# The second block of the input projection joins at step 5 in place of step 9, and its norm is put to the products

## The chip, the cores and the metric

The kernel runs on one core of a Trainium2 chip. The metric is the device time of one launch in microseconds (us). Before the change it is 2964.63 us, the median of three runs from 2958.12 to 2965.66. All traces here are of one profiled execution each.

## The reference, cut to what matters

One layer of a streaming encoder runs over 2128 tokens: 64 sample frames of a running stream, 16 meta tokens and 2048 prompt frames. What the change touches is the head of the layer:

```
h = x * rsqrt(mean(x*x) + EPS) * norm_mix_g        # one norm per token, one gain per feature
p = h @ W_in                                       # 1024 -> 2832 columns
q, k, v (attention) | lx, lg (RG-LRU) | gq, gk, gv, glr, gog (GLA) = split(p)
```

Then differential attention, the RG-LRU recurrence and the GLA recurrence work on their columns, `W_out` joins them, and a gated feed-forward network (FFN, 2816 wide, with a causal convolution) follows. A norm is one number per token, so it can be put either to `h` before the product or to the columns (or rows) of the product behind it.

## The kernel before, in words

Every matmul is done in three parts: each operand is split into a rounded high half and the rest (`hh`, `hl` for h; `whi`, `wlo` for a weight), and hh·whi, hl·whi and hh·wlo are added up in PSUM. A block of h has eight pieces of 128 features, so a unit (128 columns of `W_in` by one block) is 24 matmuls.

**W_in.** The 17 tiles of tokens (80 and 16 times 128) form six blocks, `WBLOCKS`, of 336, four times 384, and 256 tokens. The columns of `W_in` form 19 units, `UNITS` (line 87): eight `f` units for the recurrences' columns (stored to LGT), one `g` unit (three weight parts, GVR, tokens as rows), four `f` units of K, four of Q, and two `t` units of V (two weight parts, tokens as rows). `win` (from line 602) goes through steps; step s works on unit s mod 19. `WSTART` (line 94) says at which step a block joins, and a block stays for 19 steps. Blocks 0, 2, 4 use one pair of h tiles and join at steps 0, 22, 44; blocks 1, 3, 5 use the other and join at 9, 31, 53. A step with two live blocks puts one weight part to both. There are 72 steps.

**Weights.** Each step's part is loaded from HBM into one of two `raw` tiles (`w_load`), then split (`w_split`, lines 244 to 270): ScalarE writes `whi` (line 154), VectorE (line 160) or GpSimd (line 260, two of three) writes `wlo`. There are three slots of whi and wlo (`NW = 3`), so the `g` unit holds all three while it runs. All loads and stores are issued by SyncE (lines 148 and 151).

**Norms.** Block 0 uses `first_rows`: hh is x times the gain (line 496), hl the rest (497), squares are made on ScalarE (381) and added on VectorE (383), and the norm is put to the products later: `row_scale` for `g` and `t` units, `col_scale` for `f` units, so that block 0's `f` products leave PSUM by a VectorE multiply (`columns`, line 518), and the other blocks' by a ScalarE copy (520). All other blocks use `norm_in`: squares, adds on GpSimd, `rsqrt_rows` (lines 396 to 406), and then `normed` (438 to 445), which writes the scaled y and splits it into hh and hl. The raw x of a block lies in a single buffer (tile `x` of pool `xp`), so the next block's x is loaded (`load_x`) when the one before has been read for the last time. The norm of block i is begun by `win` three steps ahead or more: for i of 2 and above at the step after block i-2 has left, and for block 1 at step 1.

**Order.** Three streams (dense work, attention, recurrences) are written out by `Flow.run`, and the tile scheduler places their instructions on the engines by priority: attention and recurrences stand ahead of dense work by 30000 and 16000, `boost` puts a norm's instructions ahead by 50000, and block 0's by `FIRST`, 100000. Each engine then runs its own list strictly in that order. The recurrences' first chunk needs block 0's units 0 to 8, the attention its K, Q and V.

**After W_in.** W_out and the FFN of two groups of 512 tokens run beside the rest of the attention and the recurrences, and a last group of 1104 tokens runs alone.

Of the kernel before, what the change touches and what calls it, by code (L numbers as in the profile page):

```python
# [16 lines left out]
ALU = mybir.AluOpType  # L17
# [26 lines left out]
TILES = [(0, XW)] + [(XW + P * i, P) for i in range(SEQ // P)]  # L44
# [20 lines left out]
WBLOCKS = [[0, 1, 2], [3, 4, 5], [6, 7, 8], [9, 10, 11], [12, 13, 14], [15, 16]]  # L65
# [16 lines left out]
for _name, _w in (("gm", 8), ("gf", 8), ("gl", 8), ("lcw", 8), ("lcb", 2), ("lab", 2), ("lxb", 2), ("ll", 2), ("lsc", 6), ("lsh", 2),  # L82
# [6 lines left out]
UNITS = [("f", 1536), ("f", 1664), ("f", 1792), ("f", 1920), ("f", 2048), ("f", 2176), ("f", 2576), ("f", 2704),  # L89
         ("g", 2304)] + [("f", 512 + P * i) for i in range(4)] + [("f", P * i) for i in range(4)] + [("t", 1024), ("t", 1280)]  # L90
GVK = ((0, 3), (3, 6), (6, 8))


WSTART = [9 * (i % 2) + i // 2 * (len(UNITS) + 3) for i in range(len(WBLOCKS))]
WSTEPS = max(WSTART) + len(UNITS)


# [41 lines left out]
def tile_hymba_step(ctx, tc, xT, xkT, cache_v, wi, wo, wu, wg, wd, par, sgla, c_msk, yT_p, yT_s, nkT_p, nv_p, lh_p, lc_p, gs_p, fc_p,  # L139
                    nkT_s, nv_s, lh_s, lc_s, gs_s, fc_s):  # L140
    nc = tc.nc
# [5 lines left out]
    def ld(out, in_):  # L147
        nc.sync.dma_start(out=raw32(out), in_=raw32(in_))
# [138 lines left out]
    FIRST = 100000  # L287
# [70 lines left out]
    def boost(gen, off):  # L358

        on = off  # L360
        while True:
            tc.cur_priority -= on
            c = next(gen, "end")
            tc.cur_priority += on
            if c == "end":
                return
            on = off
            if isinstance(c, tuple):
                c, on = c[0], off * (off == FIRST)
            yield c  # L370
# [89 lines left out]
    x_ahead = {}  # L460

    def load_x(i, first=lambda: None):
        if i < len(WBLOCKS) and i not in x_ahead:
            n, tok0 = width(WBLOCKS[i]), TILES[WBLOCKS[i][0]][0]
            x_ahead[i] = xp.tile([P, KT, n], F32, tag="x", name="xt")
            step = 4 if i else 2
            for k in range(0, KT, step):
                ld(out=x_ahead[i][:, k:k + step], in_=xT[k:k + step, :, tok0:tok0 + n].rearrange("k p c -> p k c"))
                if k == 0:
                    first()  # L470

    def norm_in(i, H):
        load_x(i)
        n = width(WBLOCKS[i])
        x = x_ahead[i]
        acc = ev.tile([P, WMAX], F32, tag="acc", name="acc", bufs=1)
        for k in range(KT):
            add_square(acc, k, x[:, k], ev, True)
            if k % 2:
                yield 1000  # L480
        rb = []
        yield from rsqrt_rows(acc, n, ev, rb)
        yield from normed(rb, "gm", lambda k: x[:, k], ev, H)
        load_x(i + 1)

    row_scale, col_scale = {}, []

    def first_rows(H):

        x = x_ahead[0]  # L490
        blk = WBLOCKS[0]
        n = width(blk)
        acc = ev.tile([P, WMAX], F32, tag="acc", name="acc", bufs=1)
        for k in range(KT):
            hk, lk = H[0][:, k], H[1][:, k]
            nc.scalar.activation(out=hk, in_=x[:, k], func=AF.Copy, scale=pr("gm", k))
            nc.vector.scalar_tensor_tensor(out=lk, in0=x[:, k], scalar=pr("gm", k), in1=f(hk), op0=ALU.mult,
                                           op1=ALU.subtract)
            add_square(acc, k, x[:, k], ev)
        cuts = [(TILES[t][0], TILES[t][1]) for t in blk]  # L500
        ps = ps_t.tile([P, 4], F32, tag="t", name="ps_sq")
        for j, (o, w) in enumerate(cuts):
            nc.tensor.matmul(ps[:w, j:j + 1], lhsT=acc[:, o:o + w], rhs=ones[:, 0:1], start=True, stop=True)
        r = ev.tile([P, 4], F32, tag="r", name="r", bufs=2)
        row_norms(r, ps, cuts)
        for j, (t, (o, w)) in enumerate(zip(blk, cuts)):
            row_scale[t] = r[:w, j:j + 1]
        dg = ev.tile([P, WMAX], F32, tag="sq", name="dg", bufs=NSQ)
        pb = yield from spread(r, dg, cuts, ps_t, "t")
        rb = mp.tile([P, NMAX], F32, tag="pc", name="rb", bufs=2 * NPC)  # L510
        nc.vector.tensor_copy(rb[:, :n], pb[:, :n])
        col_scale.append(rb[:, :n])
        load_x(1)

    def columns(out, blk, ps):

        if blk[0] == 0:
            nc.vector.tensor_tensor(out, ps, col_scale[0], ALU.mult)
        else:
            nc.scalar.activation(out=out, in_=ps, func=AF.Copy)  # L520

# [19 lines left out]
    def put_q(h):  # L541
        def put(blk, tok0, n, ps):
            e = ev.tile([P, 2, WMAX], F32R, tag="e2", name="e_q", bufs=2)
            if blk[0] == 0:
                e1 = ev.tile([P, WMAX], F32, tag="ef", name="e_q1", bufs=3)
                columns(e1[:, :n], blk, ps[:, :n])
                ps = e1
            rounded(e[:, 0, :n], ps[:, :n], scale=-0.125)
            nc.vector.scalar_tensor_tensor(out=e[:, 1, :n], in0=ps[:, :n], scalar=-0.125, in1=f(e[:, 0, :n]),
                                           op0=ALU.mult, op1=ALU.subtract)  # L550
            st(QHL[h, :, :, :, tok0:tok0 + n].rearrange("l m d c -> (m d) l c"), e[:, :, :n])
        return put
# [55 lines left out]
    def win():  # L608
        H, norms = {}, {}
        for s_ in range(WSTEPS):  # L610
            u = s_ % len(UNITS)
            kind = UNITS[u][0]
            for i, blk in enumerate(WBLOCKS):

                if s_ == max(0, WSTART[i - 2] + len(UNITS)) if i >= 2 else s_ == i:
                    (H[i],) = h_tiles([width(blk)], hp, (f"hh{i % 2}_", f"hl{i % 2}_"))
                    norms[i] = boost(norm_in(i, H[i]), 50000) if i else boost(first_rows(H[i]), FIRST)
                if s_ == WSTART[i]:
                    yield from norms.pop(i)
            live = [i for i in range(len(WBLOCKS)) if WSTART[i] <= s_ < WSTART[i] + len(UNITS)]  # L620
            ranges = unit_parts(kind)
            wt = w_take(("in", s_), len(ranges))
            wd_ = unit_width(kind)

            def wview(k, l):
                for (a, b), pair in zip(ranges, wt):
                    if a <= k < b:
                        return pair[l][:, (k - a) * wd_:(k - a + 1) * wd_]
            for i in live:
                blk = WBLOCKS[i]  # L630
                b0 = TILES[blk[0]][0]
                for t in [None] if kind == "f" else blk:
                    if t is None:
                        c0, n = 0, width(blk)
                    else:
                        c0, n = TILES[t][0] - b0, TILES[t][1]
                    ps = ps_w.tile([P, NMAX], F32, tag="w", name="ps_w")
                    for k in range(KT):
                        for i3, (pa, pb) in enumerate(((0, 0), (0, 1), (1, 0))):
                            hx = H[i][pb][:, k, c0:c0 + n]  # L640
                            wx = wview(k, pa)
                            st_, sp_ = (k == 0 and i3 == 0), (k == KT - 1 and i3 == 2)
                            if t is None:
                                nc.tensor.matmul(ps[:, :n], lhsT=wx, rhs=hx, start=st_, stop=sp_)  # L644
                            else:
                                nc.tensor.matmul(ps[:n, :wd_], lhsT=hx, rhs=wx, start=st_, stop=sp_)  # L646
                        if k % 2 == 1:
                            w_pump()
                            if k == KT - 1:
                                if t is None:  # L650
                                    puts[u](blk, b0, n, ps)
                                else:
                                    puts[u](t, ps)
                            yield 6 * (n if t is None else wd_) * 0.425
                            yield from beside(norms)
                lg_done[i] = lg_done[i] or {(WSTART[i] + x) % len(UNITS) for x in range(s_ - WSTART[i] + 1)} >= set(range(9))
                win_done[i] = s_ == WSTART[i] + len(UNITS) - 1
            w_used(len(ranges))
            if s_ == 1:
                setup2()  # L660
            if s_ == 3:
                cached_keys()
                sample_masks()
# [315 lines left out]
    class Unit:  # L979
# [16 lines left out]
        def width(self, ti, ci):  # L996
            k0, kn = self.chunks[ci]
            return min(kn, self.n0 - k0) if not self.X and ti == 0 else kn
# [639 lines left out]
```

## Time and profile before

| | |
|---|---|
| median of three runs | 2964.63 us |
| profiled execution: time, span | 2966.77 us, 2965.0 us |
| mean granted TensorE clock | 0.979 |
| last matmul of W_in starts | 800.9 us |

In a row of instructions the columns are: start in us from the span's start, duration in us, engine, line, operation, out<-in, shapes, how many instructions the row merges, and in brackets the idle time of the engine before it with what ended it. PE is the matmul engine (TensorE), DVE is VectorE, ACT ScalarE, POOL GpSimd, SPq SyncE's queue. In a row of stretches: its length, the busy time of each engine with the number of instructions, the granted clock of TensorE (1.00 is 2.4 GHz, 0.5 would be 1.2 GHz throughout), the share of DMA and GB/s. In a row of groups: mean ns of one after the bar and the comma, then idle time before the group by releaser.

### The profile page before, as it was taken

The page shows a single profiled execution, that of the slowest core. Times are in us where ns is not written, and L with a number is a line of the kernel's source. Part 1 is how long each engine was busy: PE and PEld are TensorE (multiplying, and loading weights), DVE is VectorE, ACT ScalarE, POOL GpSimd, SP SyncE. Part 2 cuts the span into 40 slices and gives each one's busy share as a digit, 9 for nine tenths or more (in the row PEclk, how much of TensorE's full clock was granted, in tenths as well). Part 3 has the DMA queues.
Part 4 walks back from the last instruction along what each step waited for, and adds up shares of the span by engine and source line. Part 5 has one row for each costly group of instructions (what it writes and reads, how often), then busy time and mean ns, then how long its engine had stood idle before and what let it go on. Part 6 is the DMA issues. An engine that isn't in the chain of part 4 may idle for free.

```text
span 2965.0 us, 44672 instructions
## 1 busy us (share of the span) xinstructions
PE 2846.8 (96%) x16031; PEld 2508.9 (85%) x16031; DVE 1942.6 (66%) x3779; ACT 1140.1 (38%) x2589; POOL 864.2 (29%) x1212
## 2 busy tenths in 40 slices
PE   7999999999899999999999999999999999999998
PEld 7988899989877787787787888888989998999997
DVE  7677685788879989979979766444454333333335
ACT  5454554555555455455444433111222121212122
POOL 4435534444435445444424221100110000000001
PEclk9999999999998999999998999999999999999998
DMA  7775574655796787787775565675222222222222
GB/s 233 208 210 148 175 225 139 196 181 188 237 336 216 250 261 246 230 261 266 262 265 171 188 204 193 243 287 197 73 86 86 86 86 86 86 86 86 86 86 105
DMA packets 277931, 537.44 MB, mean 181 GB/s; under 512 B 31014, under 2 KB 170030, under 8 KB 277710
## 3 DMA queue, kind: packets, MB, share of 16 engines
q1 hardware_dynamic: 277566, 534.58, 54.7%
q8 instruction: 127, 2.08, 0.3%
q14 instruction: 94, 0.77, 0.1%
q10 hardware_dynamic: 144, 0.01, 0.0%
HBM read 382.74 MB, written 151.76 MB: 180 GB/s over the span
## 4 chain that ended last, share of the span: by engine, by line
PE 72%; DVE 15%; DMA 5%; issue 3%; ACT 3%; POOL 2%; SPq 1%; POOLq 0%; ACTq 0%; DVEq 0%
PE pu L1302 15%; PE pd L1369 15%; PE pg L1302 14%; PE pd L1437 6%; PE ps_w L644 5%; PE ps_w L646 4%; PE ps_o L1169 3%; DVE pc L1103 3%; PE ps_sc L1062 2%; PE ps_sc L1055 2%; PE ps_pt L1154 2%; DVE NB L1064 1%; PE ps_r L894 1%; DMA raw<-in_wi 1%; DVE cc L1326 1%
## 5 line engine op out<-in xcount | busy, mean ns | idle before, releaser
L260 POOL TENSOR_TENSOR wlo<-raw,whi 128x1024 fp32r<-128x1024 f32 (+1 forms) x104 | 248.1, 2387 | 315.8 <-ACT whi L154 263.9
L1326 DVE SCALAR_TENSOR_TENSOR cc<-uh,prm,cc 128x512 f32<-128x512 f32 (+4 forms) x264 | 168.3, 645 | 256.4 <-ACT cc L1324 253.4
L1065 ACT ACTIVATE pc<-ps_sc,NB 128x512 f32<-128x512 f32 (+6 forms) x400 | 224.8, 563 | 285.7 <-DVE NB L1064 244.6
L1369 PE MATMUL pd<-gh,whi 128*128 128x512 f32 (+2 forms) x880 | 317.7, 363 | 12.3 <-DVE x L1375 10.6
L1375 DVE TENSOR_TENSOR x<-x,pd 128x512 f32<-128x512 f32 (+2 forms) x320 | 195.8, 617 | 200.3 <-PE pd L1369 199.0
L1302 PE MATMUL pu<-h2h,whi 128*128 128x512 f32 (+2 forms) x880 | 319.9, 364 | 7.1 <-ACT h2h L154 2.6
L1302 PE MATMUL pu<-h2l,whi 128*128 128x512 f32 (+2 forms) x880 | 318.0, 362 | 3.6 <-POOL h2l L443 2.7
L1302 PE MATMUL pu<-h2h,wlo 128*128 128x512 f32 (+2 forms) x880 | 317.4, 361 | 0.0
L1302 PE MATMUL pg<-h2h,whi 128*128 128x512 f32 (+2 forms) x880 | 315.4, 358 | 1.7 <-DMA whi<-WS 1.7
L1302 PE MATMUL pg<-h2h,wlo 128*128 128x512 f32 (+2 forms) x880 | 315.7, 359 | 0.0
L1302 PE MATMUL pg<-h2l,whi 128*128 128x512 f32 (+2 forms) x880 | 315.2, 358 | 0.0
L1369 PE MATMUL pd<-gl,whi 128*128 128x512 f32 (+2 forms) x880 | 314.0, 358 | 0.0
L1369 PE MATMUL pd<-gh,wlo 128*128 128x512 f32 (+2 forms) x880 | 313.9, 357 | 0.0
L1319 ACT ACTIVATE uh<-pu 128x336 f32<-128x336 f32 (+3 forms) x132 | 59.3, 465 | 556.9 <-PE pu L1302 556.3
L644 PE MATMUL ps_w<-hh,whi 128*128 128x384 f32 (+2 forms) x768 | 257.7, 338 | 16.1 <-ACT whi L154 10.9
L1064 DVE TENSOR_REDUCE NB<-ps_sc 128x1 f32<-128x512 f32 (+6 forms) x400 | 209.0, 529 | 79.8 <-PE ps_sc L1062 78.8
L644 PE MATMUL ps_w<-hl,whi 128*128 128x384 f32 (+2 forms) x768 | 258.2, 337 | 0.5 <-DVE hl L160 0.5
L644 PE MATMUL ps_w<-hh,wlo 128*128 128x384 f32 (+2 forms) x768 | 254.8, 334 | 0.3 <-DVE wlo L160 0.3
L157 POOL TENSOR_SCALAR gh<-cc 128x336 fp32r<-128x336 f32 (+3 forms) x132 | 68.4, 520 | 468.8 <-DVE cc L1339 376.2
L154 ACT ACTIVATE whi<-raw 128x1024 fp32r<-128x1024 f32 (+2 forms) x160 | 165.9, 1037 | 101.6 <-DMA raw<-in_wi 31.3
L1369 PEld LDWEIGHTS pd<-gh,whi 128*128 128x128 f32 x880 | 166.3, 189 | 36.9 <-DVE x L1375 13.1
L1302 PEld LDWEIGHTS pu<-h2h,whi 128*128 128x128 f32 x880 | 168.6, 192 | 30.0 <-issue 3.0
(330 smaller groups left out, 7126.4 us busy)
## 6 DMA issues: line engine op xcount, KB each, us to landing
wlo<-WS SPq DMA_DIRECT2D x148, 512.0 KB, 4.3
whi<-WS SPq DMA_DIRECT2D x148, 512.0 KB, 4.5
raw<-in_wi SPq DMA_DIRECT2D x74, 512.0 KB, 4.5
WS<-whi SPq DMA_DIRECT2D x74, 512.0 KB, 5.1
WS<-wlo SPq DMA_DIRECT2D x74, 512.0 KB, 6.3
Kc<-KHL SPq DMA_DIRECT2D x48, 512.0 KB, 5.3
V<-VHL SPq DMA_DIRECT2D x48, 512.0 KB, 5.2
Q<-QHL SPq DMA_DIRECT2D x64, 256.0 KB, 4.3
```

Source lines behind the costliest of these rows:

```text
L154: nc.scalar.activation(out=out, in_=in_, func=AF.Copy, scale=scale)
L260: nc.gpsimd.tensor_tensor(out=lo[:, :n], in0=t[:, :n], in1=f(hi[:, :n]), op=ALU.subtract)
L644: nc.tensor.matmul(ps[:, :n], lhsT=wx, rhs=hx, start=st_, stop=sp_)
L646: nc.tensor.matmul(ps[:n, :wd_], lhsT=hx, rhs=wx, start=st_, stop=sp_)
L1064: nc.vector.tensor_reduce(NB[:qw, ti, m, ci:ci + 1], ps[:qw, :kt_], AX.X, ALU.min)
L1065: nc.scalar.activation(out=pv_[m][:qw, :kt_], in_=ps[:qw, :kt_], func=AF.Exp, scale=-1.0, bias=NB[:qw, ti, m, ci:ci + 1], accum_out=SS[:qw ...
L1103: nc.vector.scalar_tensor_tensor(out=p0, in0=p0, scalar=u.R[:qw, ti, 0, ci:ci + 1], in1=p1, op0=ALU.mult, op1=ALU.add)
L1302: nc.tensor.matmul(ps[:, :n], lhsT=w_[wi_][:, k * P:(k + 1) * P], rhs=hx, start=(k == 0 and i3 == 0), stop=(k == KT - 1 and i3 == 2))
L1326: nc.vector.scalar_tensor_tensor(out=cc[:, :m], in0=uh[:, w:w + m], scalar=cw[w], in1=cc[:, :m], op0=ALU.mult, op1=ALU.add)
L1369: nc.tensor.matmul(ps[:, :n], lhsT=w_, rhs=g_[:, o:o + n], start=(j == 0 and i3 == 0), stop=(j == len(gts) - 1 and i3 == 2))
L1375: nc.vector.tensor_tensor(x2[b, ct], x2[b, ct], ps[:, :n], ALU.add)
L1437: nc.tensor.matmul(ps[:, :n], lhsT=w_, rhs=g_, start=(k == 0 and i3 == 0), stop=(k == KT - 1 and i3 == 2))
```

## The change

`WSTART` puts blocks 1, 3 and 5 at steps 5, 27 and 49 in place of 9, 31 and 53; with that there are 68 steps. Block 1 gets `first_rows` too: its hh and hl are made from x and the gain alone, its adds of squares run on VectorE, its `f` products leave PSUM by `columns`' VectorE multiply, and its norms of rows and columns (`r`, `rb`) are kept until its last unit. The boost of block 1 stays at 50000. `load_x(2)` is called at the end of `first_rows` of block 1.

```
-WSTART = [9 * (i % 2) + i // 2 * (len(UNITS) + 3) for i in range(len(WBLOCKS))]
+WSTART = [5 * (i % 2) + i // 2 * (len(UNITS) + 3) for i in range(len(WBLOCKS))]
...
-    row_scale, col_scale = {}, []
-
-    def first_rows(H):
-
-        x = x_ahead[0]
-        blk = WBLOCKS[0]
+    row_scale, col_scale = {}, {}
+
+    def first_rows(i, H):
+
+        x = x_ahead[i]
+        blk = WBLOCKS[i]
...
-        cuts = [(TILES[t][0], TILES[t][1]) for t in blk]
+        cuts = [(TILES[t][0] - TILES[blk[0]][0], TILES[t][1]) for t in blk]
...
-        col_scale.append(rb[:, :n])
-        load_x(1)
+        col_scale[blk[0]] = rb[:, :n]
+        load_x(i + 1)
...
-        if blk[0] == 0:
-            nc.vector.tensor_tensor(out, ps, col_scale[0], ALU.mult)
+        if blk[0] in col_scale:
+            nc.vector.tensor_tensor(out, ps, col_scale[blk[0]], ALU.mult)
...
-            if blk[0] == 0:
+            if blk[0] in col_scale:
                 e1 = ev.tile([P, WMAX], F32, tag="ef", name="e_q1", bufs=3)
...
-                    norms[i] = boost(norm_in(i, H[i]), 50000) if i else boost(first_rows(H[i]), FIRST)
+                    norms[i] = boost(norm_in(i, H[i]), 50000) if i > 1 else boost(first_rows(i, H[i]), 50000 if i else FIRST)
```

## Rows read from the trace of the kernel before

**Rows 1.** The page, busy time of each engine over the span
```profile
PE 2846.8 (96%) x16031; PEld 2508.9 (85%) x16031; DVE 1942.6 (66%) x3779; ACT 1140.1 (38%) x2589; POOL 864.2 (29%) x1212
```

**Rows 2.** The table of stretches, by stage
```profile
800.00:1620.00 820.00, 773.24 (x3772) 629.71 (x3772) 720.39 (x1390) 420.64 (x973) 345.86 (x438) 0.96 0.76 253
1620.00:2965.00 1345.00, 1324.39 (x7396) 1171.43 (x7395) 624.64 (x1130) 310.52 (x614) 165.09 (x378) 0.99 0.37 131
```

**Rows 3.** The table of stretches, four tens of microseconds near the start
```profile
20.00:30.00 10.00, 8.79 (x56) 8.28 (x55) 9.68 (x20) 5.94 (x13) 8.93 (x10) 1.00 0.68 222
40.00:50.00 10.00, 10.00 (x59) 9.73 (x58) 2.91 (x8) 3.75 (x7) 4.73 (x3) 0.83 0.82 241
60.00:70.00 10.00, 4.05 (x16) 3.74 (x17) 8.69 (x15) 6.56 (x13) 6.30 (x5) 0.74 0.48 139
70.00:80.00 10.00, 10.00 (x57) 9.63 (x56) 7.05 (x18) 6.68 (x16) 5.96 (x8) 0.92 0.97 334
```

**Rows 4.** The timeline of PE, its idle times from 22 to 76 us
```profile
24.15 0.38 PE L318 MATMUL ps_lam<-lam_p,ones 64*128 64x2 f32 x2 [0.70 <-DVE rb L511]
...
39.47 0.45 PE L725 MATMUL ps_r<-xc,prm 128*128 128x83 f32 x2 [1.08 <-DVE xc L713]
...
53.36 0.35 PE L646 MATMUL ps_w<-whi,hh 128*80 128x272 f32 x1 [1.12 <-ACT whi L154]
...
63.96 0.42 PE L644 MATMUL ps_w<-hh,whi 128*128 128x336 f32 x1 [4.10 <-ACT whi L154]
...
66.86 0.38 PE L808 MATMUL ps_r<-ident,gvr 128*16 128x128 f32 x1 [1.99 <-DMA gvr<-GVR]
```

**Rows 5.** The timeline of PE, first matmuls of two units that follow each other
```profile
80.69 0.33 PE L644 MATMUL ps_w<-hh,whi 128*128 128x384 f32 x1
...
84.88 0.31 PE L644 MATMUL ps_w<-hh,whi 128*128 128x336 f32 x1
```

**Rows 6.** Groups of instructions, shapes apart, from 0 to 310 us
```profile
L260 POOL TENSOR_TENSOR wlo<-raw,whi 128x1024 fp32r<-128x1024 f32 x17 | 41.1, 2416 | 31.0 <-ACT whi L154 31.0
L154 ACT ACTIVATE whi<-raw 128x1024 fp32r<-128x1024 f32 x28 | 29.4, 1050 | 13.1 <-DMA raw<-in_wi 6.9 <-PE ps_w L644 5.2 <-PE ps_w L646 0.9
...
L381 ACT ACTIVATE sq<-xt 128x384 f32<-128x384 f32 x21 | 10.2, 512 | 0.8 <-POOL acc L383 0.8
...
L497 DVE SCALAR_TENSOR_TENSOR hl<-xt,prm,hh 128x336 fp32r<-128x336 f32 x8 | 4.4, 563 | 3.7 <-ACT hh L496 3.7
L496 ACT ACTIVATE hh<-xt,prm 128x336 fp32r<-128x336 f32 x8 | 4.2, 562 | 0.6 <-DMA xt<-in_xT 0.6
L518 DVE TENSOR_TENSOR e_lgt<-ps_w,rb 128x336 f32<-128x336 f32 x8 | 3.8, 500 | 0.0
...
L383 DVE TENSOR_TENSOR acc<-acc,sq 128x336 f32<-128x336 f32 x7 | 3.5, 500 | 0.1
```

**Rows 7.** The timeline of ACT, when block 1's x is there
```profile
18.87 0.52 ACT L381 ACTIVATE acc<-xt 128x384 f32<-128x384 f32 x1 [3.48 <-PE ps_sq L503]
21.36 1.06 ACT L154 ACTIVATE whi<-raw 128x1024 fp32r<-128x1024 f32 x1 [1.14 <-DMA raw<-in_wi]
```

**Rows 8.** The timeline of DVE from 20 to 62 us
```profile
24.13 1.34 DVE L518 TENSOR_TENSOR e_lgt<-ps_w,rb 128x336 f32<-128x336 f32 x3
...
53.45 2.77 DVE L438 SCALAR_TENSOR_TENSOR y<-xt,prm,acc 128x384 f32<-128x384 f32 x3
...
58.29 0.60 DVE L438 SCALAR_TENSOR_TENSOR y<-xt,prm,acc 128x384 f32<-128x384 f32 x1
```

**Rows 9.** Timelines of SPq, POOL, PE and ACT: block 3's load, squares and norm
```profile
245.72 0.92 SPq L148 DMA_DIRECT2D xt<-in_xT  x2
...
266.83 1.06 POOL L383 TENSOR_TENSOR acc<-acc,sq 128x384 f32<-128x384 f32 x1
...
321.38 0.72 PE L396 MATMUL ps_sq<-ones,acc 128*128 128x1 f32 x6
...
340.92 0.48 ACT L406 ACTIVATE acc<-ps_nb 128x384 f32<-128x384 f32 x1
```

## The prediction, made before the changed kernel was run

> **What bounds the kernel now.** I read the page first, then the table of stretches, then PE's idle times one by one, then the groups. The page shows PE busy for 2846.8 of 2965.0 us [rows 1]; no other engine is near. The change takes no matmul away and adds none: each block still passes 19 units, and block 1's norm costs PE the same few small products in either form. So only PE's idle time and the stretches with a low granted clock can be won or lost. From 1620 us on PE is busy for 1324.4 of 1345.0 us [rows 2] with the FFN; attention that ends there somewhat later costs nothing. From 800 to 1620 us 46.8 us are idle at a clock of 0.96 [rows 2], but the change acts there only through the order. What it acts on directly is the start of W_in and the joining of blocks.
>
> **The start before.** PE pauses 0.70 us at 24.2, 1.08 at 39.5, 1.12 at 53.4, 4.10 at 64.0 and 1.99 at 66.9 us [rows 4]. The tens of microseconds around these have a clock of 0.83, 0.74 and 0.92 [rows 3], which is part of each ten at the lower level, 1.2 GHz. At 1.00 the same columns would have taken 10 x (0.17 + 0.26 + 0.08) = 5.1 us less. With the last four pauses, 8.3 us, 13.4 us lie in this stretch. The reason is seen in the releasers: whi is late twice, because ScalarE, which runs its list in order, stands at other work, and block 0 alone gives PE little to go on with.
>
> **The change part by part** (us; below zero is faster).
>
> *Steps 5 to 8 with two blocks: -9.6.* Three `f` units and three `g` tiles of block 1 come into this stretch. A unit of 384 columns takes 84.88 - 80.69 = 4.19 us [rows 5]; a `g` tile, 24 matmuls of 272 columns, is estimated from it at 4.19 x 272 / 384 = 2.97. That is 3 x 4.19 + 3 x 2.97 = 21.5 us of work which is ready where PE paused. A weight part that lasted one unit then lasts two, so three parts split ahead cover twice the delay of ScalarE; the pauses at 39.5 and 53.4 should go with their clock. At the end of the `g` step something stays: it holds all three weight slots, so the next split starts late. I leave one split there, 1.05 us [rows 6], the pause for gvr, 1.99 [rows 4], and the 0.8 us of clock from 70 to 80 [rows 3]. 13.4 - 3.8 = 9.6 goes. Bounds: all 13.4, or nothing, if the pauses only move behind the new units. Block 0's later units, and with them the recurrences' `g` part and the first attention, come 21.5 us later; what hides this is the dense work, which has to be done anyway.
>
> *Block 1's rows at step 1: +3.* They stand 50000 ahead of dense work, without the pauses that `norm_in` leaves. In place of squares on ScalarE and adds on GpSimd there are on ScalarE eight copies and eight squares, on VectorE eight hl and seven adds. At 336 columns a copy takes 0.562, hl 0.563 and an add 0.500 us; a square at 384 takes 0.512 [rows 6]. Scaled by 384/336 to 0.64, 0.64 and 0.57, this is 8 x (0.64 + 0.51) = 9.2 us on ScalarE and 8 x 0.64 + 7 x 0.57 = 9.1 on VectorE, from 18.87, when ScalarE first takes up block 1's x [rows 7], to about 28. Queued behind it: whi of a later step, which ran at 21.36 [rows 7], and block 0's evictions, which ran from 24.13 [rows 8]. PE's fourth unit needs a PSUM buffer from those evictions (there are three), so it starts up to 28.0 - 24.1 = 3.9 us later, and with a piece of low clock like that of 40 to 50 us, 1.7, it is 5.6. Lower bound 0: x may have been there before 18.87 (ScalarE waited for a buffer, not for x), and evictions may slip in between. I take 3, nearer to the upper end, since both lists are full.
>
> Three y in a row took 2.77 us beside a GpSimd split, a single one 0.60 [rows 8]. The Trainium skill, SBUF — State Buffer, section Who interferes with whom, says that a VectorE instruction with two SBUF inputs contends with a GpSimd instruction that reads SBUF, and that the loser waits for the whole instruction. By this rule hl and the adds of block 1, with two SBUF inputs each, would wait for one GpSimd split in that stretch, 2.4 us, and the sum would be -0.2 in place of -2.6; against that, the GpSimd adds leave this stretch, which speaks for the smaller number.
>
> The tens from 20 to 30 us had PE busy for 8.79 and a clock of 1.00; a pause of 4.10 us was followed by 0.74 [rows 3, 4]. The Trainium skill, TensorE: Matmul & The Clock Gate, section What's actually happening, has the throttled state as the default, which activity releases. By this a longer pause at 24 us would cost its 1.7 us of clock too, and the sum would be -0.9; the rows leave it open, so it stands in the upper bound alone.
>
> *x of block 2 is loaded some 35 us earlier: 0.* Two more issues stand on SyncE's queue among the weight loads. The DMA share of 20 to 30 us is 0.68 [rows 3], and two raw tiles are filled ahead. Uncovered it would be the load's own time: 1024 x 384 x 4 bytes, 1.57 MB, at the 222 GB/s of that stretch [rows 3] are 7 us.
>
> *Block 1's columns by VectorE: +1.* Sixteen evictions (eight LGT, four K, four Q) of 0.500 x 384/336 = 0.57 us [rows 6] add 9.1 us to VectorE; twelve of them leave ScalarE. Three in a row took 1.34 us beside a GpSimd split [rows 8], so they aren't held by it. Bounds 0 and 9.1; VectorE is not the bound there (2.91 and 7.05 busy of 10 from 40 and from 70 us, [rows 3]), hence 1.
>
> *Four steps fewer: -1.* Four loads of 512 KB, four whi of 1.05 and four wlo, of 2.4 us on GpSimd [rows 6], go. None of it bounds PE where two streams run beside; bounds -2 and 0.
>
> *Block 3 joins at step 27 in place of 31: +4.* x has one buffer, so block 3's x is issued only when block 2 has been normed, at 245.7, and its squares are added up at 266.83 + 1.06 = 267.9 [rows 9]. Before, the norm begins at 321.4 [rows 9], and nobody waited for the squares. After, both events keep their place against step 22, but the join is four steps earlier. From the load on PE has about one unit of block 2, its three units alone and its three `g` tiles: 4 x 4.19 + 3 x 2.97 = 25.7 us of dense work, until 271.4, more by what attention puts between. The norm needs from the squares to the spread rows 340.9 - 321.4 = 19.5 us [rows 9] at the pace of before, and about 1.5 for the first h: 288.9. So block 3 is late by 288.9 - 271.4 = 17.5 at worst, and by nothing if the boosted norm runs without pause and attention stretches PE's work. Step 27 is the `g` unit, which holds all three weight slots, so the next step's work can't fill the hole; attention can. I take 4. Block 5 joins at an `f` unit, where the next part can be split: 0.
>
> Sum: -9.6 + 3 + 0 + 1 - 1 + 4 = -2.6. The profiled execution took 2966.77 us, 1.77 around its span and 2.14 above the median of the runs. 2966.77 - 2.6 = 2964.2, and the median 2964.63 - 2.6 = **2962.0**.
>
> **Rivals.** *Faster:* the new rows fit in (0), the whole 13.4 goes, block 3 is in time: -13.4 - 2 + 1 = -14.4, 2950.2. For it speaks that VectorE's 9.68 of 20 to 30 us [rows 3] is partly GpSimd's doing; against it the full lists above. *Slower:* the wait moves to block 3's join. Its price is 17.5 plus a low clock of 3.4 (as from 60 to 80 us, [rows 3]), with the rest of the sum -6.6: +14.3, 2978.9. It decides from the point where block 3's first h comes later than block 2's last `g` tile. For it speaks the single buffer and the held slots, against it attention in that stretch. *No gain:* the pauses of 40 to 67 us come back behind the new units, since the recurrences' start, which makes ScalarE late, moves with them: +3 + 1 - 1 + 0 - 3 = 0, 2964.6.
>
> **How the numbers follow.** Forecast 0.37, faster 0.25, slower 0.24, no gain 0.14. A measurement of this kernel tells about 0.3%, 8.9 us, from no change. The order of all work up to 1620 us is made anew, and the idle time of 800 to 1620 [rows 2] can move by some 7 us either way; hence the ends 2950.2 - 7 = 2943 and 2978.9 + 2 = 2981, and the forecast's own range is 2953 to 2971. Faster by over 0.3%: four fifths of the faster case and a quarter of the forecast's, 0.20 + 0.10 = 0.30. Slower: most of the slower case and a little of the others, 0.26. Within: 0.44.
>
> **What would show it.** PE from 36 to 85 us: fewer pauses than four and a clock nearer 1.00. From 22 to 30 us: a pause of 3 to 5 us in front of the fourth unit, its releaser an eviction or wlo. ScalarE's whi of that unit later than 21.4. Block 3's first `g` tile right behind block 2's last, or a pause with hh as its releaser. Busy PE within 10 us of 2846.8. The prediction is wrong in its steps if the start is as long as before, or if the difference sits behind 800 us.

## The result and the profile after

The changed kernel took 2982.03 us (median of five, 2977.56 to 2990.72) beside 2965.66 us for the kernel before; the ratio is 1.0059, interval 1.004 to 1.0077. Forecast were 2962.0 and a range up to 2981, with "slower" as the least likely of the three. The profiled execution of after took 2990.72 us, the longest of the five, so its trace shows some 9 us more than the median.

The page's busy times of after, beside [rows 1]:

```profile
PE 2855.4 (96%) x16031; PEld 2515.2 (84%) x16031; DVE 1936.9 (65%) x3797; ACT 1132.3 (38%) x2572; POOL 850.8 (28%) x1199
```

The matmuls are the same 16031. PE is busy for 8.6 us longer than before and idle for 15.3 us longer (2988.9 - 2855.4 = 133.5 against 118.2). The table of stretches by stage, of after (the last two rows answer to [rows 2]):

```profile
0.00:75.00 75.00, 58.35 (x326) 56.45 (x327) 50.50 (x113) 39.27 (x74) 27.04 (x34) 0.93 0.68 228
75.00:320.00 245.00, 225.37 (x1456) 213.55 (x1455) 182.86 (x416) 106.53 (x290) 95.56 (x113) 0.96 0.60 173
320.00:800.00 480.00, 460.00 (x3009) 433.40 (x3007) 355.91 (x746) 249.26 (x613) 206.23 (x234) 0.98 0.61 185
800.00:1620.00 820.00, 764.82 (x3743) 621.92 (x3742) 699.53 (x1351) 413.00 (x955) 347.67 (x432) 0.95 0.77 252
1620.00:2965.00 1345.00, 1337.25 (x7452) 1182.12 (x7451) 632.53 (x1146) 316.37 (x626) 162.21 (x375) 1.00 0.37 131
```

and its first three rows of the kernel before:

```profile
0.00:75.00 75.00, 57.78 (x333) 54.90 (x333) 52.18 (x120) 40.89 (x79) 34.14 (x41) 0.93 0.74 235
75.00:320.00 245.00, 229.34 (x1494) 217.64 (x1492) 174.04 (x409) 115.21 (x325) 100.63 (x125) 0.97 0.63 182
320.00:800.00 480.00, 462.02 (x3045) 435.24 (x3043) 371.30 (x731) 252.81 (x602) 218.48 (x232) 0.99 0.61 190
```

The first 75 us are no better than before (58.35 busy against 57.78 at the same 0.93), and every stage from 75 to 1620 us has less busy time and a lower clock ([rows 2] for the one from 800 us on). The FFN from 1620 on only runs later.

**The start.** PE's idle times in after, beside [rows 4], in the timeline of PE:

```profile
26.28 0.39 PE L644 MATMUL ps_w<-hh,whi 128*128 128x336 f32 x1 [3.48 <-DVE e_lgt L518]
34.63 0.80 PE L503 MATMUL ps_sq<-ones,acc 128*128 128x1 f32 x6 [1.03 <-DVE acc L383]
56.18 0.72 PE L725 MATMUL ps_r<-xc,prm 128*128 128x83 f32 x2 [4.27 <-DVE xc L713]
73.66 0.35 PE L646 MATMUL ps_w<-whi,hh 128*80 128x272 f32 x1 [0.80 <-ACT whi L154]
83.67 0.28 PE L808 MATMUL ps_r<-ident,gvr 128*16 128x128 f32 x1 [1.60 <-DMA gvr<-GVR]
94.30 0.42 PE L644 MATMUL ps_w<-hh,wlo 128*128 128x336 f32 x1 [1.27 <-DVE wlo L160]
```

The table of stretches of after, beside [rows 3]:

```profile
20.00:30.00 10.00, 6.52 (x35) 6.35 (x34) 9.18 (x18) 6.94 (x13) 4.92 (x4) 0.86 0.40 131
50.00:60.00 10.00, 5.73 (x24) 5.42 (x24) 7.25 (x20) 0.46 (x1) 3.81 (x3) 0.73 0.44 131
60.00:70.00 10.00, 10.00 (x60) 9.97 (x59) 4.37 (x8) 4.83 (x9) 0.54 (x1) 0.93 0.74 229
```

Read the three together. The four pauses of before from 39 to 67 us, 8.3 us, are replaced by 4.27 + 0.80 + 1.60 + 1.27 = 7.9 us, each some 17 to 30 us later: the first matmul of the recurrences, the whi behind it, gvr and a split. They moved with the units that they belong to; the low clock went with them (0.73 from 50 to 60 us, 0.74 from 60 to 70 before). The new pause of 3.48 us at 26.28 stands in front of the fourth unit, with an eviction as its releaser, as forecast (3 to 5). Its price in clock is in the row from 20 to 30 us, 0.86.

The timeline of DVE, ACT and POOL of after shows who was in front, beside [rows 7, 8]:

```profile
22.56 1.99 ACT L154 ACTIVATE whi<-raw 128x1024 fp32r<-128x1024 f32 x2
23.15 0.55 DVE L383 TENSOR_TENSOR acc<-acc,sq 128x384 f32<-128x384 f32 x1
25.64 1.33 DVE L518 TENSOR_TENSOR e_lgt<-ps_w,rb 128x336 f32<-128x336 f32 x3
25.73 2.36 POOL L260 TENSOR_TENSOR wlo<-raw,whi 128x1024 fp32r<-128x1024 f32 x1
26.88 1.62 DVE L383 TENSOR_TENSOR acc<-acc,sq 128x384 f32<-128x384 f32 x1
31.68 2.38 POOL L260 TENSOR_TENSOR wlo<-raw,whi 128x1024 fp32r<-128x1024 f32 x1 [1.29 <-ACT whi L154]
32.05 2.43 DVE L383 TENSOR_TENSOR acc<-acc,sq 128x384 f32<-128x384 f32 x1 [0.46 <-ACT sq L381]
34.41 0.49 DVE L518 TENSOR_TENSOR e_lgt<-ps_w,rb 128x336 f32<-128x336 f32 x1
```

whi came 1.2 us later than before, the evictions 1.5. The add of 0.55 us took 1.62 and 2.43 us beside the two GpSimd splits, and PE's 1.03 us at 34.63 wait for the second of them, while the evictions out of PSUM kept their 0.44 each. The Trainium skill, SBUF — State Buffer, section Who interferes with whom, has a VectorE instruction with two SBUF inputs contend with a GpSimd instruction that reads SBUF, for ports that one of them holds alone; these rows agree, since each of the two adds ends 0.4 us behind the end of the split beside it (28.50 and 34.48 against 28.09 and 34.06).

**Block 3's join** cost no pause of its own. The timeline of PE has its first `g` tile right behind block 2's last:

```profile
316.94 0.29 PE L646 MATMUL ps_w<-wlo,hh 128*128 128x272 f32 x1
317.06 0.42 PE L646 MATMUL ps_w<-whi,hh 128*128 128x272 f32 x2
```

### The profile page after: what moved, and what is told of

It is laid out like the page before. It is cut to its first block, busy times and chain, and to the rows that moved or that the text cites. A ratio compares the mean times of both kernels' runs of the same rounds, so it can differ in the third digit from the quotient of the medians.

```text
span 2988.9 us, 44663 instructions
## 1 busy us (share of the span) xinstructions
PE 2855.4 (96%) x16031; PEld 2515.2 (84%) x16031; DVE 1936.9 (65%) x3797; ACT 1132.3 (38%) x2572; POOL 850.8 (28%) x1199
## 4 chain that ended last, share of the span: by engine, by line
PE 51%; DVE 7%; DMA 1%; issue 1%; ACT 1%; POOL 0%; SPq 0%; POOLq 0%; ACTq 0%; DVEq 0%
PE pu L1302 14%; PE pd L1369 14%; PE pg L1302 14%; PE pd L1437 5%; PE ps_o L1169 2%; DVE pc L1103 1%; PE ps_pt L1154 1%; PE ps_sc L1062 1%; PE ps_sc L1055 1%; DVE NB L1064 1%; DVE BD L889 1%; DVE x L1375 1%; DVE cc L1326 1%; DVE y L438 0%; PE ps_r L894 0%
## 5 line engine op out<-in xcount | busy, mean ns | idle before, releaser
L157 POOL TENSOR_SCALAR pc<-pc,fr 128x512 f32<-128x512 f32 (+4 forms) x200 | 158.2, 809 | 129.1 <-DVE fr L1085 113.4
```

The costliest lines, as they stand in the source:

```text
L157: nc.gpsimd.tensor_scalar(out, in_, s, 1.0, ALU.mult, ALU.mult)
```

## The experiments

`WSTART` is the list of the steps at which the six blocks join. To see where a kernel falls behind, TensorE's matmuls were counted in the order in which they ran, each at the time usual for its shape over all traces; the lag at a point is by how much later than the profiled run of before a kernel has begun the same amount of work. It takes no account of what is put beside what. One execution says this to some 4 us either way only: three kernels whose TensorE order is that of after up to 800 us lag +2.3, -4.4 and -4.6 us at 375 us, and two with that of before -8.0 and -7.6. Times are medians, with ratios to the kernel before of the same series.

### The change taken apart

Rows alone, all joins where they were:

```
-WSTART = [5 * (i % 2) + i // 2 * (len(UNITS) + 3) for i in range(len(WBLOCKS))]
+WSTART = [0, 9, 22, 31, 44, 53]
```

> Block 1 keeps step 9 (and blocks 3 and 5 steps 31 and 53); only its rows change: norm put to the products. Theory A (the blocks that join early make the loss, above all block 5 five steps behind block 4): within 5 us of before, 2961 to 2971. Theory B (the rows: VectorE full from 19 to 35 us and sixteen evictions more): slower by most of the 17 us, 2976 to 2985. Theory C (no single part; any new order of the work costs some us): anywhere from 2955 to 2985. In the trace A and B both want the pause in front of the fourth unit (3.5 us after, 0.3 before), since the rows stand at step 1 in both.

Measured 2942.52 us, 0.9918 [0.9902, 0.9933]: 23 us faster.

Rows and block 1's join (`[0, 5, 22, 31, 44, 53]`):

> Block 1 at step 5 with the new rows, blocks 3 and 5 at 31 and 53 as before. Theory A: within 5 us of before, 2960 to 2971, and the lag behind before at equal PE work stays under 6 us up to 600 us. Theory B: 2976 to 2985, as with the whole change. Theory C: anywhere from 2955 to 2985.

Measured 2967.85, 1.0006 [0.9993, 1.0018]: what theory A expected.

With block 3's join too (`[0, 5, 22, 27, 44, 53]`):

> Blocks 1 and 3 at steps 5 and 27 with the new rows, block 5 at 53 as before. Theory A: 2966 to 2974, since block 5 joins nine steps behind block 4 again, and no lag comes up between 530 and 610 us; if block 3's join were the cost, 2976 to 2985. Theory B: 2976 to 2985. Theory C: anywhere.

Measured 2975.41, 1.0023 [1.0012, 1.0034].

All joins of the change, block 1's norm as before:

```
+norms[i] = boost(norm_in(i, H[i]), 50000) if i else boost(first_rows(i, H[i]), FIRST)
```

> Steps 5, 27 and 49 as in the change, but block 1 with the norm in its h as before. Theory A: 2978 to 2990, as slow as the change or slower, since the norm has to be done by step 5 and all pauses of the late joins stay. Theory B: 2962 to 2972, since the rows are gone. Theory C: anywhere.

Measured 2969.56, 1.002 [1.0008, 1.0032]. This lies where theory B had it (2962 to 2972) and not A, but B wanted the rows alone at 2976 or more, and they gained. A wanted them within 5 us of before. So neither theory holds over the four kernels. The steps from one kernel to the next are large and don't add up, so the order itself had to be tested.

### Nudges that change no work

The pattern by which a wlo goes to GpSimd or VectorE runs over all weights in turn. The change has four parts fewer in W_in, so it stands four places earlier at everything behind:

```
-            j = wq["n"]
+            j = wq["n"] + (0 if key[0] == "in" else 46)
```

(46 is four places earlier, since the pattern repeats after 50.)

> The kernel before, with one thing else: behind the weights of W_in, the pattern that gives about two thirds of the wlo to GpSimd and the rest to VectorE starts four places earlier, which is where it stands in the changed kernel (which has four parts fewer ahead of it). No work is added or removed. Theory O (what differs behind the start is the order alone, and any nudge moves it by some 5 to 20 us): the time moves by more than 5 us from 2965, either way, with the difference between 800 and 1620 us. Theory E (the early join and the rows have prices and gains of their own, and the order hardly matters): 2965 within 4 us.

Measured 2978.39, 1.0061 [1.0045, 1.0077]: no work was added, and it is as slow as the changed kernel. (The page has POOL x1213 and DVE x3778 beside 1212 and 3779: one wlo of 160 goes to GpSimd in place of VectorE.)

The changed kernel with 4 in place of 46, which puts the pattern back:

> The changed kernel with that pattern put back to where it stood before (four places later). Theory E: as the changed kernel, about 2980 within 4 us. Theory O: away from 2980 by more than 5 us; a part of the loss of 13 to 20 us at 800 to 1620 us goes, and 2965 to 2972 would say that the loss came from the pattern alone. The loss at 540 to 611 us (some 13 us) lies ahead of the first of these parts on TensorE and should stay under both.

Measured 2975.98, 1.005 [1.0035, 1.0065].

The rows alone, with 46:

> The kernel with block 1's new rows and all joins where they were, which took 2942.5, with the pattern four places earlier. Theory E: 2942 within 4 us, since the rows' gain is their own. Theory O: the gain of 23 us is mostly luck of the order between 1240 and 1620 us, and 10 us or more of it go: 2952 to 2965.

Measured 2960.62, 0.9994 [0.9983, 1.0004]: nearly all of the gain over the written kernel before is gone.

Block 1's join alone, with the norm as before:

```
+WSTART = [0, 5, 22, 31, 44, 53]
...
+norms[i] = boost(norm_in(i, H[i]), 50000) if i else boost(first_rows(i, H[i]), FIRST)
```

> Block 1 joins at step 5 with the norm as before; blocks 2 to 5 join at 22, 31, 44 and 53 as before. The fourth of the square: neither edit 2965, rows alone 2942.5, both 2967.9. Theory E with prices that add: the early join costs 25 us, so 2990. Theory O: nothing adds up; 2950 to 2975, and not near 2990. A third, that the early join is bad only together with the rows (their work on VectorE then stands where two blocks' evictions begin): 2960 to 2966, with a pause at block 1's join, since its norm is not through by then.

Measured 2960.82, 0.9995 [0.9984, 1.0005]. The prices don't add (2990). The time fits the third case, that the early join is bad only together with the rows, and its pause is there: PE waits 3.57 us for ScalarE's hh in front of block 1's first matmul at 50.56 us. Theory O has the time too.

The other two nudges are attention's count in the written order,

```
-    flow.run((dense(), 1875e3, 0), (attention(), 560e3, 30000),
+    flow.run((dense(), 1875e3, 0), (attention(), 563e3, 30000),
```

and the pattern at a third place (12 in place of the 46 above; 16 in the changed kernel, which has four parts fewer). On the kernel before and the changed one:

> The kernel before, with attention's work counted as 563 in place of 560 thousand when the order is written, so that it is spread by half a per cent differently against the dense work. No work is added or removed. Theory O (among orders of the same work the time has a spread of some 10 us to either side, so the change's 17 us are not to be put down to its steps alone): 2950 to 2980, and over 4 us from 2962 to 2965. Theory P (the pattern of the wlo is what moves the time by 16 to 18 us, other nudges don't): within 4 us of 2962 to 2965.

Measured 2952.64, 0.9967 [0.9955, 0.9979]: theory P falls, since this nudge leaves the pattern alone.

> The changed kernel with the same nudge of attention's count. Theory O: 2955 to 2985, over 4 us from 2980, and the difference to the kernel before with the same nudge is anything from -10 to +20 us. Theory P: 2980 within 4 us, 17 above the kernel before with the same nudge.

Measured 2974.45, 1.0043 [1.003, 1.0057].

> The kernel before with the pattern of the wlo behind W_in set to a third place (12 parts further on). Theory O: 2950 to 2980, over 4 us away from at least one of 2963 and 2978 that the other two places took. Theory P (some few weights must not be VectorE's; four places earlier is a bad place and the old one a good one): one of the two values, 2963 or 2978, within 4 us. In either case the difference lies between 800 and 1640 us.

Measured 2979.63, 1.0063 [1.0045, 1.0081].

> The changed kernel with the pattern at that same third place. If the change itself costs about 13 us whatever stands behind W_in (as between the two kernels at the old place of the pattern, 2976 against 2963), it is 13 us above the kernel before at the third place, within 5. Theory O: the difference is anything from -5 to +20 us. The stretch up to 800 us should be as in the changed kernel under both, with TensorE idle for 9 to 10 us between 500 and 600 us.

Measured 2975.55, 1.0046 [1.0029, 1.0062]: four below the kernel before under that nudge, not 13 above it.

On the rows alone, and on the rows with block 1's join:

> Block 1's new rows with all joins where they were, under the nudge of attention's count (563 for 560) that took the kernel before to 2952.6. If the rows have a gain of their own (17 to 23 us at two places of the pattern), 2930 to 2938. If those two gains were luck, which theory O says of them, 2945 to 2965.

Measured 2948.83, 0.9948 [0.993, 0.9967].

> The same at the third place of the wlo pattern, which took the kernel before to 2979.6. A gain of the rows' own: 2956 to 2963. Luck: 2970 to 2985 or below 2950.

Measured 2970.77, 1.0023 [1.0011, 1.0035]. Both times fall where luck was expected. By the ratios the rows are 6 and 12 us faster than before under the same nudge: neither the whole gain nor none.

> Block 1's rows and its join at step 5, the other joins as before, under the nudge of attention's count (563 for 560). At the written order this kernel took 2967.9, against 2942.5 with the rows alone and 2976 with all three joins: block 1's join seemed to carry 25 of the 33 us that the joins cost there. Theory F (block 1's join carries most of the cost at every order): 2968 to 2976, near the 2974.5 of the changed kernel under this nudge, and 20 us or more above the 2948.8 of the rows alone. Theory L (the cost comes with the joins of blocks 3 and 5, and the 25 us were the order's luck): 2945 to 2958. Under both the lag grows between 260 and 375 us, where block 2 is alone from step 24 to 30.

Measured 2977.28, 1.0042 [1.0027, 1.0058].

> The same at the third place of the wlo pattern, where the rows alone took 2970.8 and the changed kernel 2975.6. Theory F: 2975 or more. Theory L: 2964 to 2972. The order up to 800 us is that of the kernel which took 2967.9, so TensorE's lag up to there should repeat: about +5 at 375 us, +4 at 830 us.

Measured 2971.08, 1.0023 [1.0011, 1.0034]: F at one order, L at the other.

All ratios, by order (the pattern's place as before; four places earlier; attention's count; the third place):

```
                       as before  4 earlier  attention  third place   mean
before                   1.0000     1.0061     0.9967      1.0063    1.0023
rows alone               0.9918     0.9994     0.9948      1.0023    0.9971
rows, block 1's join     1.0006        -       1.0042      1.0023
rows, all three joins    1.0050     1.0059     1.0043      1.0046    1.0050
block 1's join, old norm 0.9995        -          -           -
three joins, old norm       -       1.0020        -           -
```

In the attention column the kernel with three joins has the pattern four places earlier as well, so that pair differs in two things.

The kernel before has a spread of 27 us over orders that do the same work. Within one order the rows gain 6 to 24 us, 15 in the mean, and the joins cost 7 to 39, 23 in the mean; the change as a whole costs 8 us in the mean (-5 to +23; four pairs, standard error some 6). The measured 17 us are this and the luck of two orders. With block 1's old norm the joins cost nothing in the end (0.9995 against 1.0000) or less (1.0020 against 1.0061), so their 23 us hold on top of the rows alone (one order each). The pattern's shift alone cost the kernel before 18 us, the rows 23 and the joined kernel 3, so it has no fixed price either.

### Where the joins cost

Lags at points of the work, us (the times are those of before):

```
at                        82   260   375   482   591   653   830  1648  2878
before, mean of 4       -0.9  -5.0  -6.7  -6.5  -6.2  -6.3  -6.5  -1.1  -1.0
rows alone, mean of 4   -0.4  -5.1  -2.0  -2.7  -1.5  -8.0  -9.4  -8.8 -11.8
three joins, mean of 4  -1.8  -6.7  -1.6  +3.4 +16.1  +9.2  +6.3  +9.9  +9.9
block 1's join          -2.4  -6.5  +5.2  +3.5  +4.5  +0.8  +4.1  +3.6  +3.6
block 1's, attention    -1.2  -5.5  +3.6  +2.2  +6.7  +3.1  +8.4 +12.3 +10.7
block 1's, third place  -0.3  -7.0  +3.3  +1.7  +2.3  -1.2  +1.5  +3.7  +4.2
block 1's and block 3's -1.0  -6.8  -3.3  +1.2 +20.8 +16.6 +13.1  +8.1  +5.9
block 3 at 28           -0.2  -8.0  -1.1  +2.3 +12.9  +7.1  +6.3  +3.2  +0.8
three joins, old norm   +0.4  -5.1  +7.5  +9.8 +13.5  +7.1  +2.0  +0.8  -0.6
```

Up to 830 us the price of the joins repeats: 10, 22, 17 and 14 us from the rows alone to all three, 12, 18 and 12 to block 1's. Block 1's join pays some 7 us of it from 260 to 375 us (its lag grows by 9 to 12 us there, that of the rows alone by 3), and the rest behind 591 us, where the rows alone win 8 us and it wins next to nothing. With block 3's most of it lies between 375 and 591 us (18 us in the mean). Of that some 10 come back by 830, little more than the rows alone win there too. The joins with block 1's old norm are much where the three joins are at 591 us (13.5), but lost 13 of it before 375. Behind 830 us nothing repeats: that is the order's part.

Two kernels tested a reason for the stretch up to 591 us, that block 4 stands alone at the `g` unit of step 46 when block 3 has left. `[0, 5, 22, 28, 44, 53]`:

> Block 1's rows, and joins at 0, 5, 22, 28, 44 and 53: beside the kernel with 27 in that list, which took 2975, only block 3 joins, and leaves, one step later. Theory G (block 3's early leave is what costs: at 27 it is gone at step 46, so block 4 passes the g unit alone, with all three weight slots held, as block 0 did at step 8 before): at 28 block 3 is still there at step 46, TensorE's idle time from 500 to 600 us falls from 9 to 14 us to 2 to 5, the lag of 13 to 20 us at 540 to 611 us isn't there, and block 2 passes the g unit of step 27 alone instead, with a pause near 290 to 310 us; the time is 2960 to 2970. Theory J (two blocks joining so close after each other are what costs, through the norms): idle time in that stretch and the time as at 27, within 4 us of 2975. Theory O: the time anywhere from 2950 to 2980, but the idle time of 500 to 600 us tells G from J all the same.

Measured 2967.98, 1.0022 [1.0008, 1.0037].

`[0, 5, 22, 28, 44, 50]`:

> The changed kernel with block 3 at step 28 in place of 27 and, since block 5 needs the buffer that block 3 leaves, block 5 at 50 in place of 49. Theory G: idle time of 500 to 600 us falls from 9 to 10 us to 2 to 5, and 5 to 13 us of the changed kernel's 2980 go: 2967 to 2975. Theory J: 2980 within 4 us, idle time as in the changed kernel. Theory O alone: 2960 to 2985, with the idle time telling G from J.

Measured 2967.48, 1.0016 [1.0003, 1.0028]. Both times fall in what G expected, but the stretch does not bear it out: from 482 to 591 us they still lose 11 us each, against 13 for the changed kernel. J was nearer there. PE's idle time from 500 to 600 us, by which the two were to be told apart, is 7.6 and 6.2 us (PE busy for 92.42 and 93.83 of the 100) beside 10.0 in after (90.05): between what G wanted (2 to 5) and what J did.

What else the joins move is seen in the norms. The view of line 438 on DVE, where a block's scaled y are written, gives the first and last start of its eight y. Blocks 2, 3, 4 and 5 in the kernel before:

```profile
L438 DVE SCALAR_TENSOR_TENSOR y<-xt,prm,acc x8: 609/616/1093, 231.0 to 245.1; 128x384 f32<-128x384 f32 x8
L438 DVE SCALAR_TENSOR_TENSOR y<-xt,prm,acc x8: 608/611/614, 341.8 to 353.3; 128x384 f32<-128x384 f32 x8
L438 DVE SCALAR_TENSOR_TENSOR y<-xt,prm,acc x8: 602/606/1364, 493.3 to 500.7; 128x384 f32<-128x384 f32 x8
L438 DVE SCALAR_TENSOR_TENSOR y<-xt,prm,acc x8: 476/478/935, 595.6 to 601.4; 128x256 f32<-128x256 f32 x8
```

in after:

```profile
L438 DVE SCALAR_TENSOR_TENSOR y<-xt,prm,acc x8: 605/613/3415, 256.5 to 267.5; 128x384 f32<-128x384 f32 x8
L438 DVE SCALAR_TENSOR_TENSOR y<-xt,prm,acc x8: 604/608/1266, 312.8 to 322.3; 128x384 f32<-128x384 f32 x8
L438 DVE SCALAR_TENSOR_TENSOR y<-xt,prm,acc x8: 515/605/606, 527.7 to 544.8; 128x384 f32<-128x384 f32 x8
L438 DVE SCALAR_TENSOR_TENSOR y<-xt,prm,acc x8: 470/475/961, 571.8 to 583.2; 128x256 f32<-128x256 f32 x8
```

in the kernel with block 1's join alone:

```profile
L438 DVE SCALAR_TENSOR_TENSOR y<-xt,prm,acc x8: 604/612/3404, 251.5 to 262.5; 128x384 f32<-128x384 f32 x8
L438 DVE SCALAR_TENSOR_TENSOR y<-xt,prm,acc x8: 606/614/2628, 307.7 to 321.4; 128x384 f32<-128x384 f32 x8
L438 DVE SCALAR_TENSOR_TENSOR y<-xt,prm,acc x8: 606/616/1351, 491.7 to 498.4; 128x384 f32<-128x384 f32 x8
L438 DVE SCALAR_TENSOR_TENSOR y<-xt,prm,acc x8: 473/482/836, 597.5 to 605.1; 128x256 f32<-128x256 f32 x8
```

and blocks 4 and 5 with block 3 at step 28 (and 5 at 53):

```profile
L438 DVE SCALAR_TENSOR_TENSOR y<-xt,prm,acc x8: 601/611/1364, 509.7 to 520.3; 128x384 f32<-128x384 f32 x8
L438 DVE SCALAR_TENSOR_TENSOR y<-xt,prm,acc x8: 468/471/831, 576.1 to 592.0; 128x256 f32<-128x256 f32 x8
```

Before, the two norms of a pair are 97 and 95 us apart. After, they are 45 and 27. Block 1's join alone brings only the first pair together (45; the second stays at 99), and up to 591 us it loses only at the first place. Block 3 at 28 leaves 56 for the second pair and loses 11 us there. The table of stretches from 480 us on shows the engines at the second place, before, after and with block 1's join alone:

```profile
480.00:530.00 50.00, 48.10 (x296) 45.62 (x295) 37.11 (x62) 29.86 (x69) 26.40 (x27) 0.97 0.49 152
530.00:600.00 70.00, 69.54 (x428) 66.31 (x427) 57.13 (x121) 35.02 (x80) 33.38 (x36) 1.00 0.70 205
```

```profile
480.00:530.00 50.00, 49.35 (x286) 46.57 (x284) 20.17 (x42) 20.64 (x42) 16.03 (x12) 1.00 0.47 149
530.00:600.00 70.00, 60.71 (x358) 56.06 (x359) 62.42 (x113) 39.38 (x93) 42.34 (x45) 0.93 0.57 171
```

```profile
480.00:530.00 50.00, 50.00 (x328) 47.90 (x327) 31.09 (x65) 26.61 (x68) 23.82 (x27) 1.00 0.56 168
530.00:600.00 70.00, 66.71 (x390) 62.72 (x390) 58.12 (x104) 36.82 (x76) 32.21 (x31) 0.98 0.67 200
```

In after VectorE first has 20.17 of 50 us to do and then 62.42 of 70. PE's pauses in the second stretch are many and small, with all kinds of releasers, and the clock is 0.93:

```profile
552.74 0.51 PE L646 MATMUL ps_w<-whi,hh 128*128 128x272 f32 x1 [2.52 <-ACT e_lgt L520]
567.52 0.67 PE L431 MATMUL ps_nb<-dg,ones 128*128 128x256 f32 x2 [0.99 <-DVE dg L425]
578.40 0.44 PE L644 MATMUL ps_w<-hh,wlo 128*128 128x384 f32 x1 [1.10 <-DVE wlo L160]
586.33 0.50 PE L1055 MATMUL ps_sc<-Kc,Q 128*128 128x512 f32 x1 [1.94 <-ACT pc L1065]
```

That the crowded norms are the cause is not shown. At the second place the joins with block 1's old norm speak against it. Their blocks 4 and 5 are 29 us apart, and they lose 4 us from 482 to 591 us:

```profile
L438 DVE SCALAR_TENSOR_TENSOR y<-xt,prm,acc x8: 604/610/614, 533.4 to 542.7; 128x384 f32<-128x384 f32 x8
L438 DVE SCALAR_TENSOR_TENSOR y<-xt,prm,acc x8: 471/482/955, 571.3 to 585.1; 128x256 f32<-128x256 f32 x8
```

At the first place the loss does not go with the distance either. The first pair of after is as close as that of block 1's join alone (45), but the three joins lose 5 us from 260 to 375 us in the mean (3 to 4 in three orders, 10 under attention's count), 2 more than the rows alone, where block 1's join loses 9 to 12. Another reason fits better there: how long block 2 stands alone. With block 3 at step 27 these are steps 24 to 26; with block 3 at 28 they are 24 to 27 (7 us lost), with block 3 at 31 they are 24 to 30. At the second place it fits in part: with block 5 left at 53 and block 3 at 27, block 4 is alone for seven steps in place of three, its norm and block 5's are 30 us apart, much as in after, and 24 us are lost from 375 to 591 in place of 18. But with block 3 at 28 the loss is the same with block 4 alone for six steps or three. Many of these differences are near the 4 us of one execution, and no kernel was run that changes one of the two and nothing else. So where the loss stands is shown, and its cause is open.

## Why the prediction was wrong

- *"Steps 5 to 8 with two blocks: -9.6"* failed first. At 82 us the mean lags of before and of the three joins are -0.9 and -1.8: about 1 us was won (the rows alone have -0.4). The term took the pauses as a shortage of dense work, which 21.5 us of it would fill. They belonged to the recurrences' first matmul, whi, gvr and a split, and came back behind the new units at 7.9 us in place of 8.3. What the term left at the end of the `g` step was about right: gvr and a split, 1.60 and 1.27 us beside 1.99 and 1.05. The pause in front of the recurrences' first matmul, which it expected to go, grew from 1.08 to 4.27 us, with a clock of 0.73 in its ten. The rival "No gain" had this, though the -3 in its sum is worked out nowhere. The 13.4 to be won were also too many: in the ten from 60 to 70 us PE was busy for 4.05 us [rows 3], so that half speed could cost it 2.0 us at most, not 2.6.
- *"Block 1's rows: +3"* had the place and the size of its pause (3.48 us, the eviction as releaser). But by 82 us the rows alone are only 0.5 us behind before (-0.4 against -0.9). What nobody forecast is that the rows alone end 15 us ahead in the mean. Some 3 of it are there at 830 us; the rest lies behind, and why is open.
- *"Block 3 joins at step 27: +4"* asked only whether block 3's norm is in time for its own join. The pause at the join was looked for and did not come, so the rival "Slower" (2978.9) had nearly the time by luck: it put the loss in another place. From 260 to 830 us the mean lag goes from -6.7 to +6.3 with the joins and from -5.0 to -6.5 before, 14.5 us more, where the sum has the +4 of the join alone. This is not block 3's own: in the same three orders block 1's join alone had cost as much by 830 us (12, 18 and 12 beside 10, 17 and 14), at other places. What the shift does to the norms' distances and to the steps with one block could have been listed beforehand: 19 to 21, 28 to 30, 41 to 43 and 50 to 52 before, 19 to 21, 24 to 26, 41 to 43 and 46 to 48 after. There are as many in the middle, but in pairs with two steps between; those saved stand at the two ends. Which of this costs is open.
- *"Block 5 joins at an f unit: 0"* is not settled. Its norm came 27 us behind block 4's, but with block 5 left at step 53 it came 30 us behind and more was lost from 375 to 591 us. Over the whole kernel its join goes with 8 us in the one order where both were run (1.0050 against 1.0023).
- *"Four steps fewer: -1"* overlooked that the parts also set the pattern of the wlo behind them. That shift alone moved three kernels by +18, +23 and +3 us.
- *The order's "some 7 us either way"* was too small: 27 us between the fastest and the slowest of four orders of the kernel before. That is more than any term of the sum, and a range made with it would have held the time.
- *The terms of 0 and +1* for x of block 2 and for block 1's columns were not measured apart.
- *"Wrong in its steps if the start is as long as before, or if the difference sits behind 800 us"*: the first is so. Of the profiled pair's 24 us, 12 are there at 830 and 12 follow.

## What to carry to other kernels

Before a pause is filled with other work, look at what ends it and ask whether that moves along: here the recurrences' first matmul, whi and gvr did, and 8.3 us of pauses became 7.9. Before a stage is shifted, list all that moves with it (here the norms on VectorE and the steps with a single block), not the joint alone: some 15 us were lost in stretches that the working did not look at. And where a planner writes one order for several streams, measure the spread over nudges that change no work before a change of under 1% is put down to its steps. The rows with the old joins, 2942.5 us, are the fastest kernel of the case and beat both, but 15 us is the gain to count on, the mean over four orders.

## What the runs showed of the hardware that was not expected

Two short pauses of PE near the end of attention stand in a long stretch of low clock. Around two idle times of 3.69 and 3.11 us the clock was near its lower level, 1.2 GHz, for three tens of microseconds (0.53, 0.50 and 0.61), though PE was busy for 5.62, 5.83 and 8.90 us of them. Whether the pauses kept it low or the thin work between them, no run tells apart. The pauses of 3.48 and 4.27 us near the start left 0.86 and 0.73 in their ten and 0.93 or more in the next. The timeline of PE and the table of stretches of after:

```profile
1593.58 1.01 PE L1184 MATMUL ps_on<-ones,osq 128*128 128x1 f32 x4 [3.69 <-ACT osq L1179]
1602.57 2.07 PE L431 MATMUL ps_nb<-dg,ones 128*128 128x512 f32 x2 [3.11 <-DVE dg L425]
```

```profile
1590.00:1600.00 10.00, 5.62 (x18) 4.45 (x18) 8.33 (x16) 5.21 (x13) 4.14 (x6) 0.53 0.66 185
1600.00:1610.00 10.00, 5.83 (x11) 2.20 (x11) 9.62 (x25) 3.80 (x9) 6.59 (x7) 0.50 0.30 95
1610.00:1620.00 10.00, 8.90 (x27) 6.68 (x27) 10.00 (x16) 2.76 (x6) 5.79 (x6) 0.61 0.21 67
```
